# Block inverse of a gated DeltaNet on one Trainium2 core: doubling on TensorE replaced by 16-row forward substitution on VectorE

## Chip, cores and metric

The kernel runs on one NeuronCore of a Trainium2 chip. The metric is the device time of one execution in microseconds (us), and the time before is the median of 3 runs. The engines are named as the profile names them: PE is TensorE (PEld is its weight loads), DVE is VectorE, ACT is ScalarE, POOL is GpSimd, SP is SyncE, which issues most of the transfers.

## The reference

The program is a decoder trunk of two layers over 256 tokens of width 2048, in float32. Each layer normalises the tokens, projects them for three groups of heads (mLSTM, forgetting attention, gated DeltaNet), projects the heads' outputs back, and then runs a SwiGLU feed-forward of width 5632. A last RMSNorm with the weights `final_norm_w` ends the program. The change touches the DeltaNet and the last norm. The DeltaNet has 4 heads of width 128; the part of it that matters here is a unit lower triangular system for each head and chunk:

```
a_mat = where(strict, (beta*k) k^T * decay, 0)          # strictly lower triangular
lhs = a_mat + I
w_val = triangular_solve(lhs, v * beta, lower=True, unit_diagonal=True)
w_key = triangular_solve(lhs, k * beta * exp(gc), lower=True, unit_diagonal=True)
```

The kernel works on chunks of 128 tokens, so there are 2 chunks (c) of 4 heads (h), which is 8 matrices of 128x128 in each layer, and it forms the inverse of `lhs` (transposed) for each of the 8.

## The kernel before

**The stream of weights.** All of the projections take their weights from `wu`, in units of 128x1024 float32. `unit` (L113) loads one unit into a tile `raw` (3 buffers, issued on SP at L107), ACT rounds it to `whi` (L122), DVE subtracts to get the remainder `wlo` (L123), and PE multiplies with both (4 buffers each). `block_a` (L153) and `block_b` (L177) hold the matmuls of the projections. There are 821 such splits in the program.

**Order of the work.** The kernel is written as a data flow over tiles. A planner orders the instructions of every engine by a simulated timeline before the kernel runs, and each engine then runs its own list strictly in that order. Work of different stages therefore stands interleaved: between the matmuls of the inverse, PE's list holds matmuls of later projections.

**The inverse (L544 to L583).** `at` holds the strictly lower triangular matrices, transposed. `tt` and `tn` hold the growing inverse in both orientations, for all heads of one chunk side by side (128x512). It starts from 2x2 blocks (L556 to L558), and `for j, b in enumerate(LEVELS)` (L559) doubles the block size five times, b = 2, 4, 8, 16, 32. One doubling of one chunk is

```
ps = heads(lambda h: (at[:, c, h], tn[:, c, h]), "lx")      # 4 matmuls of 128x128
dve.tensor_tensor(out=xx[:, c], in0=ps, in1=neg_mask(j), op=MUL)
ps = heads(lambda h: (tt[:, c, h], xx[:, c, h]), "lt")      # 4 matmuls of 128x128
dve.tensor_tensor(out=tn[:, c], in0=tn[:, c], in1=ps, op=ADD)
```

and then either a 32x32-wise transpose of `tn` to `tt` on DVE (L566, for b up to 16) or 4 more matmuls `lu` and an add (L569, L570, for b = 32). A last step joins the two 64-row halves with 64x64 matmuls (L576 and L582). After it the solved systems are used (`y0`, `s1p`, `o0`, ..., L591 on).

**Tiles.** `g4` (L76) gives large tiles from three pools by tag: `gg` has 9 buffers, `gy` 8, `gd` 5. PSUM tiles of the inverse have the tag `mg`, with 2 buffers.

**Constants and the last norm.** The masks (`cst`, 1036 columns) are loaded in layer 0 through a `gg` tile and cast by POOL to `cb` (L377, L378). The class `Final` (L272) loads the weights of the last norm in two pieces of 128x1024 (L282) into tiles of the tag `raw`, that is into two of the three buffers of the weight stream; both are held until the end of the kernel.

Of the kernel before, what the change touches and what calls it, by code (L numbers as in the profile page):

```python
# [34 lines left out]
O_GQ, O_GK, O_GV, O_GZ, O_GA, O_GB = 5136, 5648, 6160, 6672, 7184, 7188  # L35

UNITS = 24 + 8 + 8 + 6 + 4 + 16 + 16 + 32 + 32 + 4 * FT + 2 * FT
LEVELS = (2, 4, 8, 16, 32)

C_M0T = 0  # L40
C_LEV = C_M0T + P
C_MST = C_LEV + P * len(LEVELS)
C_MQK = C_MST + P
C_SEL = C_MQK + P
C_END = C_SEL + 12
# [5 lines left out]
R_GB = R_CW + 48  # L51
R_AL = R_GB + 1
R_SGN = R_AL + 1
R_END = R_SGN + 1


@with_exitstack
def tile_trunk(ctx: ExitStack, tc: tile.TileContext, x: bass.AP, wu: bass.AP, prm: bass.AP,
               cst: bass.AP, fnw: bass.AP, out: bass.AP, depth: int, units: list):
    nc = tc.nc  # L60
    act, dve, pe, pool = nc.scalar, nc.vector, nc.tensor, nc.gpsimd

    cp = ctx.enter_context(tc.tile_pool(name="cp", bufs=1))
    qp = ctx.enter_context(tc.tile_pool(name="qp", bufs=1))
# [11 lines left out]
    def g4(name, dims, dt=F32, tag="gg"):  # L76
        n = int(np.prod(dims))
        w, bufs = GTAGS[tag]
        t = (dp if tag == "gd" else gp).tile([P, w], dt, tag=tag, name=name, bufs=bufs)[:, :n]
        if len(dims) == 2:  # L80
            return t.rearrange("p (a b) -> p a b", a=dims[0])
        if len(dims) == 3:
            return t.rearrange("p (a b c) -> p a b c", a=dims[0], b=dims[1])
        return t
# [39 lines left out]
        return whi, wlo  # L124

    fill = qp.tile([P, 56], F32, name="fill")
    pool.memset(fill, 0.0)
# [11 lines left out]
    cb = cp.tile([P, C_END + P], BF16, name="cb")  # L141
# [4 lines left out]
    dve.memset(ones, 1.0)  # L146
    mhalf = cp.tile([P, 16], F32, name="mhalf")
    dve.memset(mhalf, -0.5)

    def neg_mask(j):  # L150
        return cb[:, C_LEV + j * P:C_LEV + (j + 1) * P].unsqueeze(1).to_broadcast([P, 4, P])

    def block_a(l, cols, hs):  # L153

# [117 lines left out]
    class Final:  # L272
# [5 lines left out]
        def piece(self, j):  # L278
            c = PIECES[j]
            if j in (0, 2):  # L280
                self.fw.append(wp.tile([P, 1024], F32, tag="raw", name="fw", bufs=3))
                nc.sync.dma_start(out=self.fw[-1], in_=fnw[c.start:c.start + 1024].partition_broadcast(P))  # L282
            square_sum(self.ssq, j)
            for t in range(2):
                dve.tensor_tensor(out=xall[:, t, c], in0=xall[:, t, c], in1=self.weight(c), op=MUL)
# [51 lines left out]
    def mixer(l, norm, nxt):  # L337
# [41 lines left out]
        gt1, gt2 = g4("gt1", [4, S]), g4("gt2", [4, S])  # L379
# [3 lines left out]
        br, sd, rows = gt3[:, :384], gt3[:, 384:768], gt3[:, 768:]  # L383
        ps = mps("gT")
# [75 lines left out]
        for h in range(HG):  # L460
            ps = mps("dtp", "mg")
# [26 lines left out]
        for h in range(HG):  # L488
# [4 lines left out]
            ps = mps("qkt", "mg")  # L493
# [4 lines left out]
            for i in range(4):  # L498
# [8 lines left out]
                           in1=mhalf, op=ALU.pow)  # L507
# [28 lines left out]
        for h in range(HG):  # L536
            ps = mps("vt", "mg")
# [3 lines left out]
                act.activation(out=zz[:, c, h], in_=ps[:, c * P:(c + 1) * P], func=AF.Copy, scale=nk[:, c, h:h + 1])  # L541


        tt, tn, xx = (g4(n, [2, 4, P]) for n in ("tt", "tn", "xx"))  # L544
        m0 = cb[:, C_M0T:C_M0T + P].unsqueeze(1).to_broadcast([P, 4, P])
        idb = ident.unsqueeze(1).to_broadcast([P, 4, P])

        def heads(fn, name):
            ps = mps(name, "mg")
            for h in range(4):  # L550
                lhsT, rhs = fn(h)
                pe.matmul(ps[:, h * P:(h + 1) * P], lhsT, rhs, start=True, stop=True)
            return ps.rearrange("p (h x) -> p h x", h=4)

        for c in range(2):
            dve.tensor_tensor(out=tt[:, c], in0=at[:, c], in1=m0, op=MUL)  # L556
            dve.tensor_tensor(out=tt[:, c], in0=tt[:, c], in1=idb, op=ADD)
            dve.transpose(out=tn[:, c].rearrange("p h x -> p (h x)"), in_=tt[:, c].rearrange("p h x -> p (h x)"))  # L558
        for j, b in enumerate(LEVELS):  # L559
            for c in range(2):  # L560
                ps = heads(lambda h: (at[:, c, h], tn[:, c, h]), "lx")
                dve.tensor_tensor(out=xx[:, c], in0=ps, in1=neg_mask(j), op=MUL)
                ps = heads(lambda h: (tt[:, c, h], xx[:, c, h]), "lt")
                dve.tensor_tensor(out=tn[:, c], in0=tn[:, c], in1=ps, op=ADD)
                if b <= 16:
                    dve.transpose(out=tt[:, c].rearrange("p h x -> p (h x)"),  # L566
                                  in_=tn[:, c].rearrange("p h x -> p (h x)"))
                else:
                    ps = heads(lambda h: (xx[:, c, h], tt[:, c, h]), "lu")  # L569
                    dve.tensor_tensor(out=tt[:, c], in0=tt[:, c], in1=ps, op=ADD)  # L570

        for c in range(2):
            ps = mps("lx2", "mg")
            lo, hi = slice(0, 64), slice(64, P)
            for h in range(4):
                pe.matmul(ps[hi, h * 64:(h + 1) * 64], at[lo, c, h, hi], tn[lo, c, h, lo], start=True, stop=True)  # L576
            x2 = xx[hi, c, :, lo]
            dve.tensor_scalar(out=x2, in0=ps[hi, 0:S].rearrange("p (h x) -> p h x", h=4), scalar1=-1.0, scalar2=None,
                              op0=MUL)
            ps = mps("lu2", "mg")  # L580
            for h in range(4):
                pe.matmul(ps[lo, h * 64:(h + 1) * 64], xx[hi, c, h, lo], tt[hi, c, h, hi], start=True, stop=True)  # L582
# [233 lines left out]
def _constants():  # L816
    c = np.zeros((P, C_END), np.float32)
    i = np.arange(P)[:, None]
    j = np.arange(P)[None, :]
    c[:, C_M0T:C_M0T + P] = np.where((j == i + 1) & (i % 2 == 0), -1.0, 0.0)  # L820
    for n, b in enumerate(LEVELS):
        m = (i // (2 * b) == j // (2 * b)) & (i // b % 2 == 1) & (j // b % 2 == 0)
        c[:, C_LEV + n * P:C_LEV + (n + 1) * P] = np.where(m, -1.0, 0.0)
    c[:, C_MST:C_MST + P] = np.where(j < i, -1e30, 0.0)
# [59 lines left out]
```

## Time and profile before

| | |
|---|---|
| median of 3 runs | 2426.42 us (2426.19 to 2427.04) |
| the profiled execution, its own time | 2425.28 us |
| its span, from the first to the last instruction | 2423.5 us |
| PE busy | 2407.1 us (99%), mean granted clock 0.999 of full speed |
| DVE busy | 1484.0 us (61%) |
| ACT busy | 1194.1 us (49%) |
| POOL busy | 75.1 us (3%) |
| data moved | 436.37 MB, mean 180 GB/s |

The profiled execution took 1.8 us more than its span and 1.1 us less than the median of the runs. A busy time is the time in which an engine has at least one instruction under way; matmuls are pipelined, so the duration of one matmul is longer than its distance to the next.

### The profile page before, as it was taken

What the parts mean: (1) busy time and instruction counts of PE and PEld (TensorE: products, weight loads), DVE (VectorE), ACT (ScalarE), POOL (GpSimd) and SP (SyncE); (2) the same over time, 40 slices, a digit from 0 to 9 for tenths busy, and PEclk for the clock granted to TensorE, in tenths of its full rate; (3) what the DMA queues carried; (4) which work ended last, traced back from release to release, by engine and by line L of the source; (5) the groups of instructions that cost most, each with busy time, mean ns of one, the idle gap of its engine ahead of it and who ended that gap; (6) DMA issues with size and microseconds to landing.
All of it is one profiled execution on the core that took longest, in us unless ns stands there. A gap on an engine that the chain in (4) does not pass through costs nothing.

```text
span 2423.5 us, 34881 instructions
## 1 busy us (share of the span) xinstructions
PE 2407.1 (99%) x13568; PEld 2105.2 (87%) x13568; DVE 1484.0 (61%) x2150; ACT 1194.1 (49%) x1871; POOL 75.1 (3%) x107
## 2 busy tenths in 40 slices
PE   9999999999999999999999999999999999999998
PEld 8888888888888888888898888889888888888887
DVE  6876655566655665466558766555665556655655
ACT  6743554554434454445566435554544344544443
POOL 0310000000000000000003000000000000000000
PEclk9999999999999999999999999999999999999999
DMA  6543445555555555556545434454656555655554
GB/s 231 178 153 131 148 168 172 182 174 191 196 196 182 189 194 200 183 187 195 190 163 180 153 133 158 156 185 149 208 185 202 195 182 184 197 196 187 182 197 170
DMA packets 121030, 436.37 MB, mean 180 GB/s; under 512 B 13728, under 2 KB 14496, under 8 KB 120864
## 3 DMA queue, kind: packets, MB, share of 16 engines
q1 hardware_dynamic: 120304, 432.99, 53.5%
q8 instruction: 106, 1.74, 0.3%
q10 hardware_dynamic: 560, 1.15, 0.1%
q14 instruction: 60, 0.49, 0.1%
HBM read 431.99 MB, written 2.10 MB: 179 GB/s over the span
## 4 chain that ended last, share of the span: by engine, by line
PE 98%; DMA 1%; DVE 1%; ACT 1%; issue 0%; SPq 0%; POOLq 0%; POOL 0%; DVEq 0%; ACTq 0%
PE pu L162 13%; PE pg L162 13%; PE pu L166 7%; PE pg L166 7%; PE dn L189 6%; PE dn L191 6%; PE dn L190 6%; PE wo L189 2%; PE wo L190 2%; PE wo L191 2%; PE fq L162 2%; PE fk L162 2%; PE gkq L162 2%; PE fk L166 1%; PE fq L166 1%; PE gkq L166 1%
## 5 line engine op out<-in xcount | busy, mean ns | idle before, releaser
L123 DVE TENSOR_TENSOR wlo<-raw,whi 128x1024 fp32r<-128x1024 f32 (+2 forms) x821 | 989.8, 1217 | 679.0 <-ACT whi L122 442.9
L122 ACT ACTIVATE whi<-raw 128x1024 fp32r<-128x1024 f32 (+2 forms) x821 | 866.4, 1056 | 903.4 <-DMA raw<-wu 447.4
L162 PE MATMUL pu<-hl,whi 128*128 128x512 f32 x1408 | 350.2, 391 | 0.0
L162 PE MATMUL pg<-hl,whi 128*128 128x512 f32 x1408 | 336.9, 391 | 0.0
L162 PEld LDWEIGHTS pu<-hl,whi 128*128 128x128 f32 x1408 | 259.0, 188 | 50.4
L162 PEld LDWEIGHTS pg<-hl,whi 128*128 128x128 f32 x1408 | 259.0, 188 | 50.2
L190 PE MATMUL dn<-wlo,hid 128*128 128x512 f32 (+1 forms) x728 | 275.8, 379 | 0.0
L191 PE MATMUL dn<-whi,hid 128*128 128x512 f32 (+1 forms) x728 | 275.6, 379 | 0.0
L189 PE MATMUL dn<-whi,hid 128*128 128x512 f32 (+1 forms) x728 | 274.1, 379 | 0.0
L166 PEld LDWEIGHTS pg<-hl,wlo 128*128 128x128 f32 x1408 | 191.0, 190 | 13.1
L166 PE MATMUL pg<-hl,wlo 128*128 128x256 f32 x1408 | 195.1, 282 | 0.0
L166 PE MATMUL pu<-hl,wlo 128*128 128x256 f32 x1408 | 183.3, 283 | 0.0
L166 PEld LDWEIGHTS pu<-hl,wlo 128*128 128x128 f32 x1408 | 175.4, 192 | 0.2
L191 PEld LDWEIGHTS dn<-whi,hid 128*128 128x128 f32 x728 | 137.0, 188 | 25.7
L190 PEld LDWEIGHTS dn<-wlo,hid 128*128 128x128 f32 x728 | 137.0, 188 | 25.6
L189 PEld LDWEIGHTS dn<-whi,hid 128*128 128x128 f32 x728 | 136.6, 188 | 25.0
L189 PE MATMUL wo<-whi,yhl 128*128 128x512 f32 (+1 forms) x320 | 112.5, 353 | 0.0
L190 PE MATMUL wo<-wlo,yhl 128*128 128x512 f32 (+1 forms) x320 | 111.9, 350 | 0.0
L191 PE MATMUL wo<-whi,yhl 128*128 128x512 f32 (+1 forms) x320 | 110.9, 348 | 0.0
L170 ACT COPY up<-pu 128x256 f32<-128x256 f32 x88 | 32.8, 373 | 121.8 <-PE pu L166 121.8
L783 DVE TENSOR_TENSOR hid<-up,hid 128x256 fp32r<-128x256 f32 x88 | 37.4, 424 | 88.7 <-ACT hid L782 88.7
L191 PEld LDWEIGHTS wo<-whi,yhl 128*128 128x128 f32 x320 | 60.6, 189 | 7.2
(352 smaller groups left out, 2943.7 us busy)
## 6 DMA issues: line engine op xcount, KB each, us to landing
raw<-wu SPq DMA_DIRECT2D x808, 512.0 KB, 4.2
raw<-wu SPq DMA_DIRECT2D x10, 420.0 KB, 3.2
xall<-x SPq DMA_DIRECT2D x3, 512.0 KB, 8.1
fw<-fnw SPq DMA_DIRECT2D x2, 512.0 KB, 4.3
out<-xall ACTq DMA_DIRECT2D x2, 512.0 KB, 2.9
out<-xall SPq DMA_DIRECT2D x2, 512.0 KB, 2.9
xall<-x SPq DMA_DIRECT2D x2, 256.0 KB, 4.3
cst<-cst SPq DMA_DIRECT2D x1, 512.0 KB, 9.5
```

The lines of the kernel that those rows point to most:

```text
L122: act.activation(out=whi[:, c], in_=raw[:, c], func=AF.Copy)
L123: dve.tensor_tensor(out=wlo[:, c], in0=raw[:, c], in1=f32(whi[:, c]), op=SUB)
L162: pe.matmul(ps, whi[:, i * P:(i + 1) * P], hs[half * 8 + i][2], start=(half + i == 0), stop=False)
L166: pe.matmul(ps[:, :S], los[2 * n + half][:, i * P:(i + 1) * P], hs[half * 8 + i][0], start=False, stop=(half == 1 and i == 7))
L170: act.copy(out=dst, in_=ps[:, S:])
L189: pe.matmul(pst[t][:, :w], hhi[:, sl], w1, start=st, stop=False)
L190: pe.matmul(pst[t][:, :w], hhi[:, sl], w2, start=False, stop=False)
L191: pe.matmul(pst[t][:, :w], hlo[:, sl], w1, start=False, stop=en)
L783: dve.tensor_tensor(out=lo, in0=up, in1=f32(hi), op=SUB)
```

## The change

Inside the inverse, only the doublings b = 16 and b = 32 are left on PE. The blocks of 16 rows are inverted on DVE, for all 8 matrices at once: four transposes of 32 partitions gather the 32x32 diagonal blocks into `a32`, masks pick the two 16x16 diagonal blocks of each (`ac`), and 15 steps of forward substitution follow, each a shuffle across partitions, a multiply and an add on 8 x w elements per partition, w = 1 to 15. The result `t16` has 16 columns for each matrix. The two doublings then multiply with right-hand sides of 16 and 32 columns only (`level`: two rounds of 8 matmuls); ACT copies the first product out of PSUM. `spread` writes the diagonal blocks, transposed, back into the 128x128 tile `tt`. The masks are multiplied into `at` beforehand (`am`, two `gy` tiles). The join of the 64-row halves keeps its matmuls, with its operands in new tiles. The weights of the last norm get `gg` tiles of their own, and the constants, now 572 columns, go through a `raw` tile. An unused tile `fill` is dropped.

```diff
-LEVELS = (2, 4, 8, 16, 32)
+LEVELS = (16, 32)
...
-                self.fw.append(wp.tile([P, 1024], F32, tag="raw", name="fw", bufs=3))
+                self.fw.append(g4("fw", [1024]))
...
-                st = g4("cst", [c1 - c0])
+                st = wp.tile([P, 1024], F32, tag="raw", name="cst", bufs=3)[:, :c1 - c0]
...
-        tt, tn, xx = (g4(n, [2, 4, P]) for n in ("tt", "tn", "xx"))
-        m0 = cb[:, C_M0T:C_M0T + P].unsqueeze(1).to_broadcast([P, 4, P])
-        idb = ident.unsqueeze(1).to_broadcast([P, 4, P])
+        tt, tn, xx = g4("tt", [2, 4, P]), g4("tn", [1024]), g4("xx", [2, 4, P])
+        am = [g4("am", [8, P], tag="gy") for b in LEVELS]
...
+        QUADS = [slice(q * 32, (q + 1) * 32) for q in range(4)]
+        pool.memset(tt, 0.0)
+        for j, m in enumerate(am):
+            dve.tensor_tensor(out=m, in0=atf, in1=bc8(cb[:, C_LEV + j * P:C_LEV + (j + 1) * P]), op=MUL)
+        for q in QUADS:
+            dve.transpose(out=a32[q], in_=atf[q, :, q])
+        dve.tensor_tensor(out=sh, in0=a32[:, :, 0:16], in1=bc8(cb[:, C_LOW:C_LOW + 16]), op=MUL)
+        dve.tensor_tensor(out=ac, in0=a32[:, :, 16:32], in1=bc8(cb[:, C_LOW + 16:C_LOW + 32]), op=MUL)
+        dve.tensor_tensor(out=ac, in0=ac, in1=sh, op=ADD)
+        dve.tensor_copy(out=t16, in_=bc8(cb[:, C_ID16:C_ID16 + 16]))
+        for j in range(15):
+            w = j + 1
+            dve.stream_shuffle(out=sh[:, :, :w], in_=t16[:, :, :w], mask=[j] * 16 + [16 + j] * 16)
+            dve.tensor_tensor(out=tmp[:, :, :w], in0=sh[:, :, :w], in1=ac[:, :, j:w].to_broadcast([P, 8, w]), op=MUL)
+            dve.tensor_tensor(out=t16[:, :, :w], in0=t16[:, :, :w], in1=tmp[:, :, :w], op=ADD)
...
-        for c in range(2):
-            dve.tensor_tensor(out=tt[:, c], in0=at[:, c], in1=m0, op=MUL)
-            dve.tensor_tensor(out=tt[:, c], in0=tt[:, c], in1=idb, op=ADD)
-            dve.transpose(out=tn[:, c].rearrange("p h x -> p (h x)"), in_=tt[:, c].rearrange("p h x -> p (h x)"))
-        for j, b in enumerate(LEVELS):
-            for c in range(2):
-                ps = heads(lambda h: (at[:, c, h], tn[:, c, h]), "lx")
-                dve.tensor_tensor(out=xx[:, c], in0=ps, in1=neg_mask(j), op=MUL)
-                ps = heads(lambda h: (tt[:, c, h], xx[:, c, h]), "lt")
-                dve.tensor_tensor(out=tn[:, c], in0=tn[:, c], in1=ps, op=ADD)
-                if b <= 16:
-                    dve.transpose(out=tt[:, c].rearrange("p h x -> p (h x)"),
-                                  in_=tn[:, c].rearrange("p h x -> p (h x)"))
-                else:
-                    ps = heads(lambda h: (xx[:, c, h], tt[:, c, h]), "lu")
-                    dve.tensor_tensor(out=tt[:, c], in0=tt[:, c], in1=ps, op=ADD)
+        def spread(src):
+
+            for q in QUADS:
+                dve.transpose(out=ttf[q, :, q], in_=src[q])
+
+        def level(m, t, x, b):
+
+            for lhs, rhs, dst in ((m, t, x), (ttf, x, None)):
+                ps = mps("lx" if dst is not None else "lt", "mg")
+                for n in range(8):
+                    pe.matmul(ps[:, n * b:(n + 1) * b], lhs[:, n], rhs[:, n], start=True, stop=True)
+                ps = ps[:, :8 * b].rearrange("p (n x) -> p n x", n=8)
+                if dst is not None:
+                    act.copy(out=dst, in_=ps)
+            return ps
+
+        dve.tensor_scalar(out=t32d[:, :, 0:16], in0=t16, scalar1=par(0), scalar2=None, op0=MUL)
+        dve.tensor_scalar(out=t32d[:, :, 16:32], in0=t16, scalar1=par(1), scalar2=None, op0=MUL)
+        spread(t32d)
+        ps = level(am[0], t16, x16, 16)
+        dve.tensor_tensor(out=t32[:, :, 0:16], in0=t32d[:, :, 0:16], in1=ps, op=ADD)
+        act.copy(out=t32[:, :, 16:32], in_=t32d[:, :, 16:32])
+        spread(t32)
+        ps = level(am[1], t32, x32, 32)
+        dve.scalar_tensor_tensor(out=t64[:, :, 0:32], in0=t32, scalar=par(2), in1=ps, op0=MUL, op1=ADD)
+        act.activation(out=t64[:, :, 32:64], in_=t32, func=AF.Copy, scale=par(3))
+        for q in (0, 2):
+            dve.transpose(out=ttf[QUADS[q], :, QUADS[q + 1]], in_=t64[QUADS[q + 1], :, 0:32])
...
-                pe.matmul(ps[hi, h * 64:(h + 1) * 64], at[lo, c, h, hi], tn[lo, c, h, lo], start=True, stop=True)
-            x2 = xx[hi, c, :, lo]
+                pe.matmul(ps[hi, h * 64:(h + 1) * 64], at[lo, c, h, hi], t64[lo, c * 4 + h], start=True, stop=True)
+            x2 = x2s[hi, c]
```

## Rows read from the trace of the kernel before

**Rows 1.** The page: the span, busy time by engine, the chain by engine.

```profile
span 2423.5 us, 34881 instructions
PE 2407.1 (99%) x13568; PEld 2105.2 (87%) x13568; DVE 1484.0 (61%) x2150; ACT 1194.1 (49%) x1871; POOL 75.1 (3%) x107
...
PE 98%; DMA 1%; DVE 1%; ACT 1%; issue 0%; SPq 0%; POOLq 0%; POOL 0%; DVEq 0%; ACTq 0%
```

**Rows 2.** PE's waits: line and releaser, us in total, times, longest us.

```profile
PE xT L250 <- DMA xall<-x: 4.4, 1, 4.4
PE dn L205 <- DVE wlo L123: 1.7, 2, 0.9
PE dn L204 <- ACT whi L122: 1.2, 1, 1.2
```

**Rows 3.** Busy by engine in the inverse of either layer: PE, PEld, DVE, ACT, POOL.

```profile
130.00:232.00 102.00, 102.00 (x650) 90.57 (x649) 70.78 (x116) 41.49 (x63) 5.60 (x6) 1.00 0.44 145
1338.00:1440.00 102.00, 102.00 (x650) 90.16 (x649) 68.18 (x106) 39.97 (x61) 3.46 (x3) 1.00 0.42 140
```

**Rows 4.** PE matmuls of the inverse by form: busy us, mean ns.

```profile
L552 PE MATMUL lt<-xx,tt 128*128 128x128 f32 x160 | 21.2, 275 | 0.0
...
L552 PE MATMUL lu<-tt,xx 128*128 128x128 f32 x32 | 4.2, 275 | 0.0
...
L576 PE MATMUL lx<-tn,at 64*64 64x64 f32 x32 | 2.7, 224 | 0.0
```

**Rows 5.** PE's timeline in the inverse: start us, us from first to last.

```profile
157.64 1.05 PE L552 MATMUL lt<-xx,tt 128*128 128x128 f32 x8
158.53 1.06 PE L552 MATMUL lx<-tn,at 128*128 128x128 f32 x8
...
224.25 0.68 PE L576 MATMUL lx<-tn,at 64*64 64x64 f32 x8
```

**Rows 6.** Weight loads by form.

```profile
L552 PEld LDWEIGHTS lx<-tn,at 128*128 128x128 f32 x160 | 19.6, 192 | 0.2
...
L576 PEld LDWEIGHTS lx<-tn,at 64*64 64x64 f32 x32 | 2.1, 134 | 0.3 <-issue 0.3
```

**Rows 7.** DVE by form: two groups of the inverse, one 128-column operation.

```profile
L564 DVE TENSOR_TENSOR tn<-tn,lt 128x512 f32<-128x512 f32 x20 | 13.7, 683 | 20.3 <-PE lt L552 20.2
...
L566 DVE STREAM_TRANSPOSE tt<-tn 128x512 f32<-128x512 f32 x16 | 11.3, 705 | 0.2
...
L676 DVE TENSOR_TENSOR mo<-mn,mo 128x128 f32<-128x128 f32 x16 | 3.6, 285 | 0.0
```

**Rows 8.** DVE's timeline: small operations, each on the result of the one before.

```profile
240.61 0.17 DVE L668 TENSOR_TENSOR mva<-mst,inv 128x8 f32<-128x8 f32 x1
240.81 0.17 DVE L669 TENSOR_TENSOR mva<-mva,inv 128x8 f32<-128x8 f32 x1
```

**Rows 9.** The page: the splits of the weights on DVE.

```profile
L123 DVE TENSOR_TENSOR wlo<-raw,whi 128x1024 fp32r<-128x1024 f32 (+2 forms) x821 | 989.8, 1217 | 679.0 <-ACT whi L122 442.9
```

**Rows 10.** DVE's timeline among the gate operations of layer 0.

```profile
58.66 0.27 DVE L413 TENSOR_SCALAR gt<-gt 12x128 f32<-12x128 f32 x1
58.86 1.21 DVE L123 TENSOR_TENSOR wlo<-raw,whi 128x1024 fp32r<-128x1024 f32 x1
59.99 0.21 DVE L414 TENSOR_SCALAR gt<-gt 12x128 f32<-12x128 f32 x1
```

**Rows 11.** The end of the chain: a transfer between the two last splits.

```profile
2401.43 1.22 DVE wlo L123
2402.67 4.91 DMA raw<-wu
```

**Rows 12.** SP's timeline at the end: the second piece of the norm weights.

```profile
2385.85 0.33 SPq L282 DMA_DIRECT2D fw<-fnw  x1
```

**Rows 13.** The page: transfers of the constants and of the weights, us to landing.

```profile
raw<-wu SPq DMA_DIRECT2D x808, 512.0 KB, 4.2
...
cst<-cst SPq DMA_DIRECT2D x1, 512.0 KB, 9.5
```

More of the change, by code (lines that the diff above doesn't have):

```diff
@@ L37 @@
 UNITS = 24 + 8 + 8 + 6 + 4 + 16 + 16 + 32 + 32 + 4 * FT + 2 * FT
-LEVELS = (2, 4, 8, 16, 32)
-C_M0T = 0
-C_LEV = C_M0T + P
-C_MST = C_LEV + P * len(LEVELS)
+LEVELS = (16, 32)
+C_LEV = 0
+C_LOW = C_LEV + P * len(LEVELS)
+C_ID16 = C_LOW + 32
+C_MST = C_ID16 + 16
 C_MQK = C_MST + P
@@ L53 @@
 R_SGN = R_AL + 1
-R_END = R_SGN + 1
+R_PAR = R_SGN + 1
+R_END = R_PAR + 4
 @with_exitstack
@@ L63, in tile_trunk @@
     cp = ctx.enter_context(tc.tile_pool(name="cp", bufs=1))
-    qp = ctx.enter_context(tc.tile_pool(name="qp", bufs=1))
     xp = ctx.enter_context(tc.tile_pool(name="xp", bufs=1))
@@ L124, in unit @@
         return whi, wlo
-    fill = qp.tile([P, 56], F32, name="fill")
-    pool.memset(fill, 0.0)
     xall = xp.tile([P, 2, D], F32, name="xall")
@@ L148, in tile_trunk @@
     dve.memset(mhalf, -0.5)
-    def neg_mask(j):
-        return cb[:, C_LEV + j * P:C_LEV + (j + 1) * P].unsqueeze(1).to_broadcast([P, 4, P])
     def block_a(l, cols, hs):
@@ L541, in mixer, with par, bc8 @@
                 act.activation(out=zz[:, c, h], in_=ps[:, c * P:(c + 1) * P], func=AF.Copy, scale=nk[:, c, h:h + 1])
-        tt, tn, xx = (g4(n, [2, 4, P]) for n in ("tt", "tn", "xx"))
-        m0 = cb[:, C_M0T:C_M0T + P].unsqueeze(1).to_broadcast([P, 4, P])
-        idb = ident.unsqueeze(1).to_broadcast([P, 4, P])
+        tt, tn, xx = g4("tt", [2, 4, P]), g4("tn", [1024]), g4("xx", [2, 4, P])
+        am = [g4("am", [8, P], tag="gy") for b in LEVELS]
+        atf, ttf, xxf = (v.rearrange("p c h x -> p (c h) x") for v in (at, tt, xx))
+        a32, t32d, t32 = (tn[:, i * S:(i + 1) * S].rearrange("p (n x) -> p n x", n=8) for i in range(3))
+        ac, t16 = (tn[:, 768 + i * P:896 + i * P].rearrange("p (n x) -> p n x", n=8) for i in range(2))
+        t64 = xxf[:, 0:4].rearrange("p n x -> p (n x)").rearrange("p (n x) -> p n x", n=8)
+        x32 = xxf[:, 4:6].rearrange("p n x -> p (n x)").rearrange("p (n x) -> p n x", n=8)
+        x16, sh = (xxf[:, 6 + i].rearrange("p (n x) -> p n x", n=8) for i in range(2))
+        tmp = t32d[:, :, 0:16]
+        def par(i):
+            return pr[:, l, R_PAR + i:R_PAR + i + 1]
+        def bc8(ap):
+            return ap.unsqueeze(1).to_broadcast([P, 8, ap.shape[-1]])
+        QUADS = [slice(q * 32, (q + 1) * 32) for q in range(4)]
[13 more added lines that the diff above has]
+            dve.tensor_tensor(out=t16[:, :, :w], in0=t16[:, :, :w], in1=tmp[:, :, :w], op=ADD)
         def heads(fn, name):
@@ L574, in mixer @@
             lo, hi = slice(0, 64), slice(64, P)
+            x2s = tn[:, 0:512].rearrange("p (c h x) -> p c h x", c=2, h=4)
             for h in range(4):
-                pe.matmul(ps[hi, h * 64:(h + 1) * 64], at[lo, c, h, hi], tn[lo, c, h, lo], start=True, stop=True)
-            x2 = xx[hi, c, :, lo]
+                pe.matmul(ps[hi, h * 64:(h + 1) * 64], at[lo, c, h, hi], t64[lo, c * 4 + h], start=True, stop=True)
+            x2 = x2s[hi, c]
             dve.tensor_scalar(out=x2, in0=ps[hi, 0:S].rearrange("p (h x) -> p h x", h=4), scalar1=-1.0, scalar2=None,
@@ L581, in mixer @@
             for h in range(4):
-                pe.matmul(ps[lo, h * 64:(h + 1) * 64], xx[hi, c, h, lo], tt[hi, c, h, hi], start=True, stop=True)
+                pe.matmul(ps[lo, h * 64:(h + 1) * 64], x2s[hi, c, h], tt[hi, c, h, hi], start=True, stop=True)
             act.copy(out=tt[lo, c, :, hi], in_=ps[lo, 0:S].rearrange("p (h x) -> p h x", h=4))
@@ L819, in _constants @@
     j = np.arange(P)[None, :]
-    c[:, C_M0T:C_M0T + P] = np.where((j == i + 1) & (i % 2 == 0), -1.0, 0.0)
     for n, b in enumerate(LEVELS):
-        m = (i // (2 * b) == j // (2 * b)) & (i // b % 2 == 1) & (j // b % 2 == 0)
+        m = (i // (2 * b) == j // (2 * b)) & (i // b % 2 == 0) & (j // b % 2 == 1)
         c[:, C_LEV + n * P:C_LEV + (n + 1) * P] = np.where(m, -1.0, 0.0)
+    k = np.arange(16)[None, :]
+    for n in range(2):
+        c[:, C_LOW + n * 16:C_LOW + (n + 1) * 16] = np.where((i // 16 % 2 == n) & (i % 16 > k), -1.0, 0.0)
+    c[:, C_ID16:C_ID16 + 16] = i % 16 == k
     c[:, C_MST:C_MST + P] = np.where(j < i, -1e30, 0.0)
@@ L855 @@
         prm[l, 32:36, R_SGN] = 1.0
+        rows = np.arange(P)
+        for n, b in enumerate((16, 16, 32, 32)):
+            prm[l, :, R_PAR + n] = rows // b % 2 == n % 2
     nc = _bacc.Bacc("TRN2", target_bir_lowering=False, num_devices=1)
```

## The prediction

> **What bounds the kernel now.** I first read the busy times and the chain on the page. PE is busy for 2407.1 of 2423.5 us and makes up 98% of the chain that ended last, while DVE is busy for 61% and ACT for 49% [rows 1]. A busy PE can still be a PE that waits between modelled ends, so the next view is the list of PE's own waits. It holds five entries; the three longest are 4.4 us at the start and 1.7 and 1.2 us at the last down-projection [rows 2], the other two are 1.1 us and less. So nothing in the middle of the program ever makes PE wait, and a microsecond of matmuls taken away there is worth a microsecond, as long as what replaces it does not make PE wait.
>
> The third view is the stretch in which the inverse lies, some 102 us in either layer. PE has no gap in it; DVE is busy for 70.8 and 68.2 us and ACT for about 41 [rows 3]. The inverse is interleaved with projections there. DVE has 31 to 34 us of idle time per layer in this stretch; that is the cover for what the change puts on it.
>
> **PE, removed.** The profile counts two records for one float32 matmul: 5 doublings, 2 chunks, 4 heads and 2 layers are 80 `lt` matmuls, and the row says x160 [rows 4]. The `lx` matmuls are as many again, and `lu` adds 32 records, so 352 go. The mean duration of 275 ns is a latency and not a price. The price is the distance: eight `lt` records begin at 157.64 and the next group at 158.53 [rows 5], which is 0.89/8 = 0.111 us each. 352 x 0.111 = **39.1 us**.
>
> **PE, added.** Two doublings of two rounds of 8 matmuls are 32 matmuls or 64 records per layer, 128 in all, each with a stationary matrix of 128x128 and 16 or 32 moving columns. The trace has no such record. The nearest rows bound it: a 128x128 record takes 0.111, a 64x64 one (0.68 - 0.22)/7 = 0.066 us [rows 4, 5]. What decides is whether the moving columns or the weights set the distance. The load of 128 columns lasts 192 ns and that of 64 columns 134 [rows 6]: 58 ns for 64 columns, so about 116 ns for the 128 beyond a fixed part. That is already the whole distance between records, and the new ones keep their 128 stationary columns. I therefore take the upper end, 0.111: 128 x 0.111 = **14.2 us** (8.4 at the lower end). The narrowness then saves nothing by itself; the gain comes from 352 records that become 128, which is 24.9 us.
>
> [...]
>
> **DVE.** Removed per layer: 26 operations of 512 columns at 0.683 us (`lx` masks, adds, first blocks; two rows of the same size as L564 stand for them) and 10 transposes at 0.705 [rows 7], 17.8 + 7.1 = 24.8 us. For the added ones the rows give a line: 8 columns 0.17 us [rows 8], 128 columns 0.285, 512 columns 0.683 [rows 7], so about 0.16 us plus 1.02 ns a column; an operation on the result of the one before starts 0.20 after one of 0.17, which is 0.03 more [rows 8]. The substitution has 45 operations on 8w columns, w = 1 to 15: 45 x 0.19 + 3 x 8 x 120 x 0.00102 = 8.6 + 2.9 = 11.5 us. The two masks of 1024 columns cost 1.22 each [rows 9], 2.4 us; 14 transposes of 256 columns some 0.44, 6.2 us; 7 operations of 128 columns 2.0 us; one of 256 columns 0.42. The sum is 22.5 us in 69 operations, 2.3 us less than the 24.8 in 36. The trace has no shuffle: I price it like any operation of its size; if it costs a second small operation for its mask, 15 x 0.17 = 2.6 us more. DVE is not the bound in either case.
>
> **PE waiting for the chain.** What is new is the shape: masks, 8 transposes, six small operations and the substitution are 2.4 + 3.5 + 1.7 + 11.5 = 19.1 us of DVE work in one dependent row before the first new matmul, where before PE and DVE took turns. Each engine runs its list in order, so if DVE ran this row without a break, no weights would be split meanwhile, and PE's list would stand at the first matmul that lacks them. 821 splits in 2423.5 us [rows 1, 9] are one each 2.95 us, and four buffers cover 11.8 us. The upper bound is 19.1 - 11.8 = 7.3 us per layer, 14.6 in all; the lower bound is nothing. The planner has not kept splits behind ready chain operations before: at 58.86 a split stands between L413 and L414, though both only need results that are there [rows 10]. With splits in between, the chain spreads over some 35 us that are full of projection matmuls. I take 0.5 us per layer, **+1 us**.
>
> **The last norm's weights.** The second piece is issued at 2385.85 [rows 12], and from then on two of the three `raw` buffers hold norm weights. The chain shows what follows: after a split at 2401.43, a transfer of 4.91 us that could only start then [rows 11], and PE's 1.7 and 1.2 us of waiting lie right behind it [rows 2]. With own buffers, the last weights come two units earlier. The `gg` tiles held the hidden values of an earlier part and are free by then. Gain between 0 and 2.9 us; I take **2.9**, since three buffers feed PE without a wait everywhere else.
>
> **Edits at nothing.** The constants: 572 instead of 1036 columns, no longer first in line with the weights, but through a `raw` buffer. A weight transfer lands in 4.2 us, the large transfer of the constants took 9.5 [rows 13]. Less traffic at the start can gain up to a microsecond or two, one lost buffer turn costs at most one unit, 2.95 us, which the four split buffers cover; I take zero. POOL's clearing of `tt` lies beside everything: POOL is busy for under 6 us of the stretch [rows 3]. Six small operations on ACT per layer, 4 us even at the 0.7 of a 512-column one, go into 60 idle us. The `gy` tiles of the masks are needed again only by the last outputs of the mixer; were they late, a transposed output would wait, not the projections.
>
> **The sum.** 2425.3 (the profiled execution) - 39.1 + 14.2 + 1 - 2.9 = 2398.5; it lay 1.1 us under the median of the runs, so **2399 us**, 1.1% faster. Its own range, from the small terms, is 2394 to 2404.
>
> **Rivals.** (a) *Narrow is cheap*: the distance follows the moving columns. At the 64x64 row's 0.066 the sum is 5.8 us lower, **2393**. For it speaks that all records shown so far have a distance in step with their moving columns too; against it, the weights row above. Chance 0.13. [...]
>
> (b) *DVE runs the chain unbroken*: PE waits up to 14.6 us in all, and the time is 2404 to **2413**. For it speaks that gate operations stand in rows of several without a split; against it [rows 10]. Chance 0.14.
>
> (c) *The substitution is slow*: the shuffle, or an operation with an inner run of a few elements, costs far more than its size says, and the chain is late for PE's first narrow matmul. The gain of 27.8 us is gone when PE waits 13.9 us per layer, that is when the unbroken row is 25.7 instead of 19.1 us, 0.40 per step operation instead of 0.256. At 0.55 the row is 32.3 us, PE waits 20.5 per layer, 41 in all, and the time is **2439**: slower. For it speaks that no row shows a shuffle; against it, that every DVE row at hand fits the line, and that splits in between and DVE's 31 idle us take much of the delay. Chance 0.07; about break-even, 0.06.
>
> [...]
>
> (d) *It moves less than it says*: if the last weights come no sooner, 2402; inside the forecast's own range.
>
> **Chances.** Forecast 0.60, (a) 0.13, (b) 0.14, break-even 0.06, (c) 0.07. Within 0.2% (4.9 us, about what a measurement of this kernel can tell from no change) lies break-even alone: faster 0.87, same 0.06, slower 0.07. The range takes in (a) with the unknown below it and (b): 2387 to 2413.
>
> **What would show it.** After the change, PE's records fall by 224, and the distance of the narrow records is 0.11 if weights bind, 0.07 or less for (a). DVE's step operations start about 0.25 us apart; a shuffle well above its size speaks for (c). PE's waits stay near 5 us at the start and lose the entries at the last down-projection; an entry at the new `lx` or a wait for `wlo` in the inverse is (b) or (c). The time between the inverse's first operation and its last shrinks. The prediction is wrong if PE's waits in the inverse reach several us per layer, or if the records' distance is not 0.11.

## The result, and the profile after

The changed kernel took 2398.12 us (median of 4 runs, 2397.10 to 2399.22), the kernel before 2426.73 us beside it (4 runs, 2426.19 to 2428.97). The ratio is 0.988 with a 95% interval of 0.9863 to 0.9898: faster by 1.2%. The forecast was 2399 us.

The page of the kernel after (its profiled execution took 2399.22 us), span and busy times:

```profile
span 2397.4 us, 34530 instructions
PE 2382.9 (99%) x13344; PEld 2081.5 (87%) x13344; DVE 1477.3 (62%) x2246; ACT 1194.7 (50%) x1879; POOL 77.2 (3%) x107
```

Beside [rows 1], the span is 26.1 us shorter. PE has 224 records less and 24.2 us less of busy time; the other 1.9 us are waits of PE. DVE has 96 instructions more (30 of them are loads of a shuffle's mask) and is busy 6.7 us less. The next view is the list of PE's waits in the kernel after:

```profile
PE xT L245 <- DMA xall<-x: 4.7, 1, 4.7
PE mv L184 <- ACT whi L123: 1.1, 1, 1.1
PE cols L431 <- ACT gt L421: 0.6, 1, 0.6
PE dtp L443 <- DVE bg L317: 0.4, 1, 0.4
```

The two entries of [rows 2] at the last down-projection are gone, and so is one of 0.4 us at the start. No entry stands at a line of the inverse (L559 to L620 now). Two small ones are new, both among the gate operations of the first layer, before 70 us; the inverse begins at 139. In the inverse itself, here by busy time per engine in layer 0, from the first mask to the sum behind the last narrow matmul (columns as in [rows 3], with the granted clock, the DMA share and GB/s at the end), PE has no gap and a granted clock of 1.00:

```profile
138.90:197.30 58.40, 58.40 (x341) 50.95 (x339) 45.45 (x119) 28.84 (x45) 3.04 (x5) 1.00 0.49 154
```

PE's timeline of the kernel after shows the narrow matmuls, each group with the record behind it (start, us from first to last, number of records):

```profile
177.78 1.85 PE L589 MATMUL lx<-tn,am 128*128 128x16 f32 x16
179.49 0.47 PE L688 MATMUL mnum<-mv,mp 128*128 128x129 f32 x2
...
189.09 1.86 PE L589 MATMUL lx<-tn,am 128*128 128x32 f32 x16
190.79 0.68 PE L684 MATMUL mkq<-mqkT 128*128 128x256 f32 x2
```

Sixteen records take 179.49 - 177.78 = 1.71 us, 0.107 each, with 16 moving columns, and 1.70 us with 32. In [rows 5] a record with 128 moving columns takes 0.111. So the distance does not follow the moving columns here; wide64 (0.108 us at 64 of them) and split64 (0.065 us for a pair of 64x64 in place of one of 128x128) below show that it goes with the stationary matrix. DVE's timeline shows the steps of the substitution, and the split of a weight unit between two of them:

```profile
153.86 0.01 DVE L568 LOAD_MASK_SELECT xx<-tn  x1
153.86 0.19 DVE L568 STREAM_SHUFFLE xx<-tn 128x24 f32<-128x24 f32 x1
154.08 0.18 DVE L569 TENSOR_TENSOR tn<-xx,tn 128x24 f32<-128x24 f32 x1
...
154.40 1.22 DVE L124 TENSOR_TENSOR wlo<-raw,whi 128x1024 fp32r<-128x1024 f32 x1
...
173.48 0.29 DVE L568 STREAM_SHUFFLE xx<-tn 128x120 f32<-128x120 f32 x1
173.81 0.28 DVE L569 TENSOR_TENSOR tn<-xx,tn 128x120 f32<-128x120 f32 x1
174.13 0.28 DVE L570 TENSOR_TENSOR tn<-tn 128x120 f32<-128x120 f32 x1
```

The starts lie 0.22 us apart at 24 columns and 0.32 to 0.33 at 120. The prediction's line (0.19 us plus 1.02 ns a column) gives 0.21 and 0.31. The mask of the shuffle costs 0.01. From the first step at 150.43 to the last at 174.13 lie 24 us with 8 splits, one each 3.0 us, about the mean rate of the kernel before (one each 2.95): the stream of weights goes on. From its first operation to its last, the inverse of layer 0 takes 73.8 us (138.96 to 212.78) in place of 104.7 (133.1 to 237.8). The transposes, in DVE's operations by form, cost what was estimated (0.44):

```profile
L582 DVE STREAM_TRANSPOSE tt<-tn 32x256 f32<-32x256 f32 x16 | 7.0, 435 | 0.2
```

Last, SP's timeline: the second piece of the last norm's weights is issued at 2170.97 and not at 2385.85 as in [rows 12].

```profile
2170.97 0.42 SPq L277 DMA_DIRECT2D fw<-fnw  x1
```

### The profile page after: what moved, and what is told of

Read it like the earlier page. It is cut to its first block, busy times and chain, and to the rows that moved or that the text cites. A ratio compares the mean times of both kernels' runs of the same rounds, so it can differ in the third digit from the quotient of the medians.

```text
span 2397.4 us, 34530 instructions
## 1 busy us (share of the span) xinstructions
PE 2382.9 (99%) x13344; PEld 2081.5 (87%) x13344; DVE 1477.3 (62%) x2246; ACT 1194.7 (50%) x1879; POOL 77.2 (3%) x107
## 4 chain that ended last, share of the span: by engine, by line
PE 97%; ACT 1%; DVE 1%; DMA 1%; issue 0%; POOLq 0%; POOL 0%; DVEq 0%; ACTq 0%
PE pu L157 13%; PE pg L157 13%; PE pu L161 7%; PE pg L161 7%; PE dn L186 7%; PE dn L184 7%; PE dn L185 7%; PE wo L184 2%; PE wo L186 2%; PE wo L185 2%; PE fq L157 2%; PE fk L157 2%; PE gkq L157 2%; PE fk L161 1%; PE fq L161 1%; PE mk L157 1%
## 5 line engine op out<-in xcount | busy, mean ns | idle before, releaser
L185 PEld LDWEIGHTS dn<-wlo,hid 128*128 128x128 f32 x728 | 137.0, 188 | 25.7
L157 PE MATMUL fk<-hl,whi 128*128 128x512 f32 x256 | 67.8, 401 | 0.0
```

Of the source, the lines that this page charges most:

```text
L157: pe.matmul(ps, whi[:, i * P:(i + 1) * P], hs[half * 8 + i][2], start=(half + i == 0), stop=False)
L185: pe.matmul(pst[t][:, :w], hhi[:, sl], w2, start=False, stop=False)
```

## The experiments

The edits are made to the kernel after, unless another is named. In kernels whose edit adds lines, the numbers behind it are larger by one to three (L590 for L589). Where kernels of different sets of runs are compared, it is by their medians; the kernel before moved between 2426.7 and 2428.1 us from set to set, so a difference of about 1 us across sets says little.

### The two parts, each alone

**before_fw**, on the kernel before: only the last norm's weights get tiles of their own.

```diff
-                self.fw.append(wp.tile([P, 1024], F32, tag="raw", name="fw", bufs=3))
+                self.fw.append(g4("fw", [1024]))
```

> The kernel before with only the last norm's weights moved to their own tiles. Theory: 2426.7 - 2.9 = 2423.8 us, ratio 0.9988, with PE's two waits at the last down-projection gone. Rival: 2426.7, ratio 1.000. If this and the run that undoes the same part in the changed kernel have the same size, the two parts of the change add up.

Measured: 2422.00 us (10 runs, 2421.71 to 2422.44) against 2427.97 (18 runs, 2425.03 to 2429.84), ratio 0.9976, interval 0.9967 to 0.9986. In the profiled execution the estimate of 2.9 us holds to the digit: the span is 2420.6 instead of 2423.5, and the entries at the down-projection are gone. In the medians it is 6.0 us. The difference lies in the runs of the kernel before. Nine of its 18 have a mean granted clock of 0.998 and take 2428.8 us on average, nine have 0.999 and take 2426.8; the profiled one, with 2425.3, is among the quickest. All ten runs of before_fw have 0.999 and lie within 0.8 us. The clock is only part of the difference, as far as its three digits tell: the nine runs at 0.999 still take 4.8 us more than before_fw, not 2.9.

**fw_raw**, the reverse: the kernel after with the last norm's weights in `raw` tiles again.

```diff
-                self.fw.append(g4("fw", [1024]))
+                self.fw.append(wp.tile([P, 1024], F32, tag="raw", name="fw", bufs=3))
```

> The changed kernel with the last norm's weights back in two of the three raw buffers. Theory (the end term of the prediction, 2.9 us): PE again waits some 2.9 us for the last two splits, so 2398.1 + 2.9 = 2401.0 us, with PE's waits at the last down-projection back in the list of waits. Rival (the last weights come no sooner, or the end is set by what follows PE): 2398 us, no such waits or no effect of them.

Measured: 2403.14 us (4 runs, 2400.87 to 2406.27), 0.9899 of before (0.9885 to 0.9912), 5.0 us more than the kernel after (3.8 if each is taken against the kernel before of its own set). Two of the four runs have a clock of 0.999 and take 2401.2 on average, two have 0.998 and take 2405.5. The first two lie 3.1 us above the kernel after, near the expected 2.9. The profiled one is of the latter. Its waits at the end, and then the stretch that follows (length, PE busy, granted clock, DMA share, GB/s):

```profile
PE dn L199 <- ACT whi L123: 1.9, 1, 1.9
...
PE dn L185 <- DVE wlo L124: 0.9, 1, 0.9
PE dn L200 <- DVE wlo L124: 0.9, 1, 0.9
...
PE dn L184 <- ACT whi L123: 0.2, 1, 0.2
```

```profile
2383.00:2386.00 3.00, 0.69 (x4) 1.00 0.28 112
2386.00:2389.00 3.00, 2.54 (x14) 0.67 0.00 0
2389.00:2392.00 3.00, 3.00 (x21) 0.76 0.00 0
2392.00:2395.00 3.00, 3.00 (x27) 1.00 0.18 71
```

After 2.3 us of 3 without work, the granted clock is 0.67 and 0.76 for 6 us. The waits sum to 3.9 us; the span is 5.5 us longer than that of the kernel after, so some 1.6 us are the clock's, as the two stretches give by themselves (2.54 x 0.33 + 3.00 x 0.24 = 1.6, an estimate). So in this execution the wait that the edit removes costs more than its own length. In the profiled execution of the kernel before, the clock was 1.00 up to 2415, so its trace could not show it. But its gaps were shorter there, 0.8, 1.2 and 0.9 us against 1.9 and 0.9 here, and the 3 us with the longest of them read

```profile
2406.00:2409.00 3.00, 1.80 (x12) 1.00 0.03 5
```

A longer wait is therefore the other part of the price of fw_raw, beside the lower clock.

### The price of a narrow record

**wide64**: the moving operand repeated to 64 columns.

```diff
-                    pe.matmul(ps[:, n * b:(n + 1) * b], lhs[:, n], rhs[:, n], start=True, stop=True)
-                ps = ps[:, :8 * b].rearrange("p (n x) -> p n x", n=8)
+                    r = rhs[:, n].unsqueeze(1).to_broadcast([P, 64 // b, b])
+                    pe.matmul(ps[:, n * 64:(n + 1) * 64], lhs[:, n], r, start=True, stop=True)
+                ps = ps.rearrange("p (n x) -> p n x", n=8)[:, :, :b]
```

> The changed kernel with the moving operand of the two doublings repeated to 64 columns instead of 16 and 32 (the same stationary matrices, same result). Theory (a full stationary load sets the distance): no change, 2398 us, 0.107 us between records at 64 columns as at 16 and 32. [...]

Measured: 2398.59 us (4 runs, 2397.98 to 2399.71), 0.988 of before (0.9865 to 0.9895): no difference from the kernel after. PE's timeline of wide64:

```profile
176.93 1.89 PE L590 MATMUL lx<-tn,am 128*128 128x64 f32 x16
178.66 0.44 PE L689 MATMUL mnum<-mv,mp 128*128 128x129 f32 x2
```

1.73/16 = 0.108 us with 64 moving columns, against 0.107 with 16 and 32: under the same stationary matrices of 128x128 the added columns cost next to nothing here.

**level_twice**: each narrow matmul issued twice, 128 records more.

```diff
+                    for _ in range(2):
                         pe.matmul(ps[:, n * b:(n + 1) * b], lhs[:, n], rhs[:, n], start=True, stop=True)
```

> The changed kernel with each matmul of the two doublings issued twice into the same place (128 more records, same result). Theory (weights set the distance, PE is the bound): 128 x 0.107 = 13.7 us more, 2411.8 us, with 0.107 us between records. [...] Second rival (PE is not the bound in this stretch): 2398.

Measured: 2420.08 us (9 runs, 2418.91 to 2425.56), 0.9972 of before (0.9963 to 0.9982). That is 22.0 us more than the kernel after, where 128 x 0.107 = 13.7 were expected. The records stand 0.109 us apart, and PE's waits in the inverse are none, so the price was right and something else came with it. The stretch of level_twice behind the third doubled group (columns as above), then the 100 us around the inverse in either layer (columns as in the result section):

```profile
196.00:200.00 4.00, 4.00 (x13) 0.64 0.00 0
```

```profile
100.00:200.00 100.00, 100.00 (x593) 88.27 (x592) 77.92 (x181) 50.85 (x92) 18.27 (x24) 0.98 0.48 153
1300.00:1400.00 100.00, 100.00 (x581) 88.49 (x580) 77.02 (x184) 49.24 (x92) 16.95 (x20) 0.95 0.47 148
```

PE was busy without a gap, yet the granted clock fell to 0.64 in the first stretch. Before it fell, PE had issued 32 narrow records on end. In layer 0 it fell so behind one of the four groups (0.93 from 192 to 196, 0.64 from 196 to 200, and 1.00 in the rest of 170 to 212). A clock of 0.98 and 0.95 over 100 us costs 2 + 5 = 7 us of PE's work, about what is missing. This was a cost that the theory did not have.

**twice_wide** asks what it hangs on: the matmuls twice, as in level_twice, and with 64 moving columns, as in wide64.

```diff
+                    r = rhs[:, n].unsqueeze(1).to_broadcast([P, 64 // b, b])
+                    for _ in range(2):
+                        pe.matmul(ps[:, n * 64:(n + 1) * 64], lhs[:, n], r, start=True, stop=True)
```

> Each matmul of the two doublings issued twice, as in the run that cost 22 us instead of 13.7 and showed a granted clock of 0.64 and 0.93 without any wait of PE, but with the moving operand repeated to 64 columns. Theory (the narrow records leave the array idle, and that let the clock fall): with 64 columns the clock stays at 1.00 and only the distance is paid, 2398.3 + 13.7 = 2412.0 us. Rival (the clock falls for another reason, such as the list of PE running dry or the loads themselves): again about 2420 us with the clock below 1.00 in the inverse.

Measured: 2412.55 us (5 runs, 2412.26 to 2413.12), 0.9943 of before (0.993 to 0.9955). The record distance and the clock of the same place:

```profile
191.84 3.68 PE L591 MATMUL lx<-tn,am 128*128 128x64 f32 x32
195.36 0.44 PE L690 MATMUL mnum<-mv,mp 128*128 128x129 f32 x2
```

```profile
196.00:200.00 4.00, 4.00 (x25) 1.00 0.00 0
```

3.52/32 = 0.110 us, the same distance, with a clock of 1.00 from 184 to 204 us, and a mean clock of 0.999 in each of the five runs against 0.993 to 0.997 in those of level_twice; 128 x 0.110 = 14.1 us, and 14.4 are measured. So level_twice lost 7.5 us to the clock. The two kernels have the same number of records at the same distance and differ in the moving columns alone, so the loss went with the narrow moving side and not with the number of records; why is not shown. In the kernel after, groups of half the length leave the clock at 1.00 (174 to 202 and 1364 to 1388 us).

### How late the substitution may be

**chain_x2, chain_x4, chain_x8**: shuffle and multiply of each of the 15 steps two, four and eight times. By the prediction's line, one such set of 30 operations is 5.7 + 2.0 = 7.7 us per layer, so they add 8, 23 and 54 us to each row. The edit of chain_x4:

```diff
+            for _ in range(4):
                 dve.stream_shuffle(out=sh[:, :, :w], in_=t16[:, :, :w], mask=[j] * 16 + [16 + j] * 16)
                 dve.tensor_tensor(out=tmp[:, :, :w], in0=sh[:, :, :w], in1=ac[:, :, j:w].to_broadcast([P, 8, w]), op=MUL)
```

> The changed kernel with shuffle and multiply of each step issued twice (30 more operations, some 7.5 us per layer, same result). The run with four issues made PE wait 8.7 us per layer at the DeltaNet's outputs for 22 us more of chain, so the chain seems to have a slack of about 22 - 9 = 13 us per layer. Theory (slack): 7.5 us are inside it, 2398 us, no PE wait. Rival (in proportion, 25 us for 22 us per layer): 2406.5 us, with the wait at the outputs.

> The changed kernel with the shuffle and the multiply of each of the 15 steps issued four times instead of once (90 more operations per layer at about 0.25 us from one start to the next, 22 us per layer, same result). Theory (splits of the weights stand between the steps, PE has other projections to do, and DVE has some 30 us of idle time per layer in the stretch and more behind it): under 2 us more, 2398 to 2400 us, no PE wait in the inverse. Rival (b/c of the prediction: the chain runs unbroken or late and PE waits for it): an unbroken row of 19 + 22 us against 11.8 us of buffered splits makes PE wait some 29 us per layer, 2456 us.

> The same with eight issues (210 more operations per layer, 52 us per layer). Theory: DVE's idle time within the inverse's own stretch is used up, but the stretch grows and takes idle time behind it; up to 10 us more, 2398 to 2408 us, DVE near 90% in the stretch. Rival (PE waits for the chain as in the prediction's case c): 19 + 52 - 11.8 = 59 us per layer, over 2500 us.

Measured: chain_x2 2398.93 us (4 runs, 2398.85 to 2399.24), 0.9886 of before (0.9871 to 0.9901), as the kernel after. chain_x4 2423.13 us (11 runs, 2421.38 to 2424.05), 0.9983 (0.9974 to 0.9992): 25 us lost, where the theory expected next to none. chain_x8 2494.08 us (4 runs, 2492.95 to 2494.83), 1.0276 (1.026 to 1.0292): slower than before, 96 us lost where the theory expected up to 10.

PE's waits, first of chain_x4, then the longest of chain_x8:

```profile
PE yT L323 <- DVE at L663: 14.7, 2, 7.4
...
PE yT L323 <- DVE yhl L206: 1.3, 2, 0.7
PE fs L443 <- DVE yhl L206: 1.3, 2, 0.7
```

```profile
PE lx L590 <- DVE tn L571: 34.2, 2, 17.4
```

In chain_x4 the first narrow matmul runs at 235.09 and not at 177.78, and PE still does not wait for it: the planner puts other projections ahead. The wait comes some 55 us later, from 290 to 298, where the DeltaNet's outputs are transposed for the projection back (`yT`) and no other work is left. Behind it the granted clock of chain_x4:

```profile
296.00:300.00 4.00, 1.52 (x6) 0.50 0.00 0
300.00:304.00 4.00, 3.35 (x16) 0.50 0.00 0
304.00:308.00 4.00, 3.93 (x16) 0.82 0.01 4
```

PE stands idle for 7.4 us, and then the granted clock is 0.50 over 8 us, in which PE is busy for 4.9. The three entries sum to 17.3 us of the 25 us lost. PE's busy time in these stretches, times what the clock lacks, is 3.1 us (0.76 + 1.68 + 0.71), and layer 1 comes to about as much; together that is an estimate of 6 of the remaining 7.7 us. The row thus has a cover of between 8 and 23 us per layer.

### The constants

**cst_gg**: the constants through a `gg` tile, as before.

```diff
-                st = wp.tile([P, 1024], F32, tag="raw", name="cst", bufs=3)[:, :c1 - c0]
+                st = g4("cst", [c1 - c0])
```

> The changed kernel with the constants (572 columns) loaded through a gg tile as before instead of a raw buffer. Theory (priced at zero in the prediction): 2398 us, within 1 us. Rival (the lost turn of a raw buffer at 39 us makes the weights late and causes PE's two new waits of 0.6 and 0.4 us in layer 0): 1 us less, 2397.1, with these waits gone; or, the early transfer of the constants delays the first weights: up to 1 us more.

Measured: 2397.09 us (4 runs, 2396.69 to 2397.38), 0.9878 of before (0.9864 to 0.9891). That is 1.0 us less than the kernel after, but the intervals overlap nearly in full. In the trace, of the two new waits at the gate operations (0.6 and 0.4 us) 0.2 is left, and 0.5 stands elsewhere. But in twice_wide, whose constants go through a `raw` tile, 0.2 is left as well:

```profile
PE cols L431 <- ACT gt L421: 0.2, 1, 0.2
```

So the trace does not tie these waits to the tile. Whether the `raw` tile costs that microsecond stays open.

### Beyond the change

**rows32**: the substitution over blocks of 32 rows (31 steps), so that only the doubling b = 32 is left on PE, and 64 narrow records more go.

```diff
-LEVELS = (16, 32)
+LEVELS = (32,)
...
-        for j in range(15):
+        for j in range(31):
...
-            dve.stream_shuffle(out=sh[:, :, :w], in_=t16[:, :, :w], mask=[j] * 16 + [16 + j] * 16)
+            dve.stream_shuffle(out=sh[:, :, :w], in_=t32[:, :, :w], mask=[j] * 32)
```

> A further step in the same direction: forward substitution over 32 rows on DVE (31 steps of 3 operations on 8w columns, w = 1 to 31), and only the last doubling left on PE. PE loses 64 records: 64 x 0.107 = 6.8 us less. DVE has per layer 48 more step operations, 93 x 0.19 + 3 x 8 x 496 x 0.00102 = 17.7 + 12.1 = 29.8 us instead of 11.5, less 4 transposes, a mask and some small operations (5 us), some 13 us more. Theory (PE is the bound, DVE's idle time takes it): 2398.1 - 6.8 = 2391.3 us. Rival (DVE or the longer chain becomes the bound): 2398 or more, with PE waits in the inverse.

Measured: 2398.68 us (4 runs, 2397.69 to 2400.19), 0.9885 of before (0.9871 to 0.9898): no gain. PE has its 64 records less and is busy 4.7 us less, but waits elsewhere. Its waits that the kernel after does not have, the busy times around the inverse (columns as in the result section), and PE's stretches around the waits of layer 0 and of layer 1 (columns as in fw_raw):

```profile
PE fs L443 <- DVE yhl L206: 3.0, 2, 1.6
PE yT L323 <- DVE yhl L206: 1.8, 2, 0.9
...
PE fv L184 <- DVE fqkT L166: 0.5, 1, 0.5
```

```profile
100.00:200.00 100.00, 100.00 (x573) 87.41 (x572) 90.49 (x231) 55.46 (x98) 18.35 (x24) 1.00 0.52 174
```

```profile
288.00:292.00 4.00, 2.39 (x15) 0.89 0.76 229
292.00:296.00 4.00, 3.87 (x12) 0.68 0.24 91
...
1480.00:1484.00 4.00, 2.69 (x16) 1.00 0.76 247
1484.00:1488.00 4.00, 4.00 (x19) 1.00 0.02 6
```

DVE is busy for 90 of 100 us (81 in the kernel after), and what it finishes late makes PE wait 5.3 us behind the inverse, 2.5 in layer 0 and 2.8 in layer 1. In layer 0 the clock falls behind the waits, which costs some 1.5 us of work; in layer 1 it stays at 1.00. Together this eats the 64 x 0.107 = 6.8 us that were to be saved.

**split64**: each narrow matmul as two of 64x64 on the two diagonal halves of the matrix, since the rest of the masked matrices is zero.

```diff
-                    pe.matmul(ps[:, n * b:(n + 1) * b], lhs[:, n], rhs[:, n], start=True, stop=True)
+                    for hf in (slice(0, 64), slice(64, P)):
+                        pe.matmul(ps[hf, n * b:(n + 1) * b], lhs[hf, n, hf], rhs[hf, n], start=True, stop=True)
```

> The changed kernel with each matmul of the two doublings split into two of 64x64, on the two diagonal halves of the array (256 records more narrow ones in place of 128, half the stationary columns each, same result). Theory (the columns of the stationary loads set the distance and loads follow one another): two of 0.055 for one of 0.107, no change, 2398 us within 1. Rival (the halves of the array work side by side, a pair in 0.06): 128 x 0.05 = 6.4 us less, 2391.7 us.

Measured: 2394.16 us (4 runs, 2393.47 to 2394.36), 0.9866 of before (0.9852 to 0.9879), 4.0 us less than the kernel after (4.9 in the span of the profiled executions); between the two expectations, nearer to the rival's. PE's timeline of split64:

```profile
177.36 1.11 PE L590 MATMUL lx<-tn,am 64*64 64x16 f32 x32
178.40 0.49 PE L689 MATMUL mnum<-mv,mp 128*128 128x129 f32 x2
...
187.80 1.12 PE L590 MATMUL lx<-tn,am 64*64 64x32 f32 x32
188.85 0.70 PE L685 MATMUL mkq<-mqkT 128*128 128x256 f32 x2
```

32 records in 1.04 us are 0.033 each and 0.065 a pair, against 0.107 for the one record that they replace; with 32 moving columns it is 1.05 us, so the moving columns make no difference here either. The 64x64 records `lx` of the join, which all read the same 64 partitions and write the other 64, stand 0.066 apart one by one [rows 5]. So a pair on different halves takes what a single one takes there, and the theory, by which a pair stood at 0.11, falls. Eight groups at 0.67 us less are 5.4 us. A part goes back at the entry of each group: the eight `mq` records ahead of the first one take 1.05 us up to its start (176.31 to 177.36) and 0.96 in the kernel after (176.82 to 177.78), and 8 x 0.09 = 0.7 us, an estimate, would leave 4.7 of the 4.9 seen in the span.

**split32** carries it on: b = 16 as four matmuls of 32x32, b = 32 as two of 64x64.

```diff
-                    pe.matmul(ps[:, n * b:(n + 1) * b], lhs[:, n], rhs[:, n], start=True, stop=True)
+                    for q0 in range(0, P, 2 * b):
+                        hf = slice(q0, q0 + 2 * b)
+                        pe.matmul(ps[hf, n * b:(n + 1) * b], lhs[hf, n, hf], rhs[hf, n], start=True, stop=True)
```

> The merge to 32 rows as four 32x32 matmuls on the diagonal quarters of each matrix, the merge to 64 rows as two 64x64 ones, against the version with two 64x64 ones at both (2394.2 us). Each record of that version stood 0.033 us behind the one before it. Theory, that this 0.033 us is the least distance between two records: four per matrix take 0.13 us in place of 0.065, over the 64 sets of the merge to 32 rows 64 x 0.065 = 4.2 us more, about 2398 us. Rival, that the loads of quarters overlap as those of halves do, and a set of four stands in about 0.04 us: 64 x 0.025 = 1.6 us less, about 2392.6 us.

Measured: 2392.47 us (4 runs, 2392.33 to 2393.53), 0.9858 of before (0.9842 to 0.9875), 1.7 us less than split64, and the quickest of all. PE's timeline of split32:

```profile
176.87 0.73 PE L591 MATMUL lx<-tn,am 32*32 32x16 f32 x64
177.52 0.49 PE L690 MATMUL mnum<-mv,mp 128*128 128x129 f32 x2
```

64 records in 0.65 us are 0.041 for a set of four: the rival's price, so 0.033 us was no least distance. The step from split64 to split32 is smaller than the width of either interval; the trace carries it, with 0.39 us less in each of the four groups of this width that are changed.

## Why the prediction was right, step by step

**PE.** The forecast was -39.1 + 14.2 = -24.9 us; PE's busy time fell by 24.2. The distance went with the stationary matrix, as the prediction chose: 0.107 us in place of the 0.111 that it took, 13.7 us in place of 14.2. The 39.1 us of the 352 removed records were not measured by themselves. Rival (a), that the distance follows the moving columns, is refuted by 16, 32 and 64 columns at one distance (0.107, 0.107 and 0.108 us). Its price of 0.066 us is reached only where the stationary matrices are made smaller, in split64 (0.065 for a pair), and there too 16 and 32 columns have one distance (1.04 and 1.05 us for 32 records). The prediction's range went down to 2387 us for an unknown below (a): no row and no run shows that term, and the narrow records stood 0.107 to 0.110 us apart in the kernel after, wide64, level_twice and twice_wide. Less was measured only with smaller matrices: in split32 four of 32x32 on different quarters take 0.041 us, 0.65/64 = 0.010 us a record.

**DVE.** The line from a few rows of before priced the step operations within 0.01 to 0.02 us, the shuffle included, and its mask costs 0.01 us instead of another 0.17. In all, DVE is busy 6.7 us less where the prediction had 2 x 2.3 = 4.6. With the line, rival (c) has no ground: break-even needed 0.40 us per operation, and it is 0.22 to 0.33 at 24 to 120 columns. What such a delay would do chain_x4 and chain_x8 show: PE waits, though first in another place than the rival named. The rival's price of a late chain was wrong too: by it, a row 6.6 us longer (25.7 in place of 19.1) loses the whole gain, but chain_x2 makes it 7.7 us longer and loses nothing.

**PE waiting for the chain, +1 us.** In the inverse it is nothing; the splits stand between the steps, as [rows 10] had suggested, and rival (b) is refuted. chain_x2 shows that there is room for 8 us more per layer. The microsecond that was allowed for is there, but as two new waits at the gate operations of layer 0, which are over before the chain begins; that the term came out is luck. Where they come from is open: cst_gg has less of them with the constants in their former tile, a change that the prediction had priced at nothing, but so has twice_wide without it.

**The last norm's weights, -2.9 us.** This is the term that was mis-sized. The mechanism is right: early issue, both waits gone, and 2.9 us less span for before_fw. In the medians it is worth 6.0 us alone and 3.8 to 5.0 us in fw_raw. fw_raw shows two reasons in one execution: the wait was longer (3.9 us), and a stretch at a lower granted clock followed it (1.6 us). For the kernel before, the mean clocks of its runs point the same way, but the runs at 0.999 lie 4.8 us over before_fw as well, so how much is the clock's and how much a longer wait stays open. The rival (d), 2402, is about what fw_raw measures (2403.1).

**The sum.** The inverse alone comes to 23.9 us from before_fw to the kernel after (2422.0 - 2398.1, across two sets of runs), to 24.8 from the kernel before to fw_raw (2428.0 - 2403.1, in one set), and to 22.6 as the whole gain less that of before_fw (28.6 - 6.0). The prediction's terms for it give 39.1 - 14.2 - 1 = 23.9. The whole was forecast at 27.4 us against the median of the runs and measured at 28.6: the last-norm term was 1 to 3 us too small, and the three ways of taking the inverse differ by as much, so the runs cannot divide the rest more finely. The mechanism is confirmed term by term; that the whole comes within 1 us is finer than these terms are known.

## What to carry to other kernels

Price a stream of small matmuls, each with a stationary matrix of its own, by the size of that matrix: under one of 128x128, narrowing the moving side from 128 columns to 16 brought a record from 0.111 to 0.107 us here, while 224 records less brought PE's busy time down by 24.2 us, and smaller matrices on separate partitions brought the same product from 0.107 to 0.065 and 0.041 us. A dependent row of small operations on VectorE cost nothing here as long as the other work of that engine stood between its steps: 7.7 us more per layer lost nothing, 23 us more lost 25 us in all; so lengthen such a row on purpose to see how far the cover goes. And a wait that looks small in one profile may cost twice as much in the median (2.9 and 6.0 us here), so its price is read from several executions.

## What the runs showed of the hardware that was not expected

- The granted clock fell without a wait of PE in level_twice: to 0.64 over 4 us behind one of the four groups of 32 records in layer 0, and to 0.98 and 0.95 over the 100 us around the inverse of either layer, with 16 or 32 moving columns; with 64, the same number of records and nearly the same distance (0.109 and 0.110 us), it is 1.00 at the same place. Why is not shown.
- Matmuls on the diagonal halves or quarters of a matrix stand closer than single ones: 0.065 us for two of 64x64, 0.041 for four of 32x32, against 0.107 for one of 128x128 and 0.066 for a single 64x64 behind another on the same partitions.
- After 7.4 us of idle time the granted clock is 0.50 over 8 us (chain_x4), and after 2.3 us of idle time in 3 us it is 0.67 and 0.76 over 6 us (fw_raw). Nearly the same waits had two prices in one execution: in rows32, 2.5 us in two waits are followed by 0.68 over 4 us in layer 0, and 2.8 us in three waits by 1.00 in layer 1.
